# A hybrid decoder step: the S5 branch's inner table T kept in a contiguous layout

## The chip, the cores and the metric

The kernel runs on one core of a Trainium2 chip. The metric is the time of one execution in device microseconds; where several executions are given, their median. The trace is one execution, taken by the hardware profiler.

## What is computed

One layer of a hybrid decoder on 512 prompt tokens with 16 meta tokens in front, and on 8 running sequences of 4 tokens. After a norm and a large projection two branches run side by side: a gated linear recurrence in 8 heads (HGRN2), and a diagonal state-space branch (S5) in 64 groups of 16 channels with 64 complex states each. Their outputs are gated and merged; an expert-retrieval mixer (PEER) follows. The change touches the S5 branch:

```python
b_bar = ((a_bar - 1.0) / lam)[..., None] * lax.complex(b_re, b_im)
bu = jnp.einsum('gpc,nlgc->nlgp', b_bar, ug)
...
_, xs = lax.associative_scan(combine, (a_seq, bu), axis=1)
y = jnp.real(jnp.einsum('gcp,nlgp->nlgc', cc, xs)) + d_skip * ug
```

## The kernel before

The S5 branch is worked in blocks of 8 tokens. For each of the 64 groups a block's 8 x 16 = 128 inputs (U) give 128 outputs in two parts: one through the state at the start of the block (table W, 128x128 per group), and one directly from the inputs of the same block (table T, 128x128 per group, lower triangular in the tokens). A third table, AT, leads from the inputs into the state.

These tables are constants of the weights. `s5_setup` (L204) makes them on the chip, in 8 octets of 8 groups, and writes them to device memory as `Td`, `Wd` and `ATd`. It is a generator in the list `fill`: `Stream.run` calls `bg.tick` and `fill.tick` after every 12 of its matmuls, and each tick runs a generator up to its next `yield`. So the program order on every engine is set at build time, the set-up's steps lie between the matmuls of the weight stream (`gps`, L469) and the heads of the recurrence, and each engine then runs its instructions in that order. Transfers are issued with `load` (L104), nearly all on SP's queue, in program order too; a transfer whose data isn't ready holds those behind it. On the same queue are the weight tiles `wraw`, two buffers deep, each of which waits until POOL (or DVE) has read the tile before out of its buffer (`wl`, L435, after ACT's cast `wh`, L434).

For one octet the set-up computes E and W on DVE (L369, L371), multiplies E with C on PE (L382), adds the skip term on DVE (L378, L383) to give a small tile T7, transposes E on PE (L387) into AT, and then places T7 eight times, moved by 16 partitions each, with eight transfers into a tile T of shape [128, 2, 8, 16, 4]: half octet, token s, channel c, group g, with the group innermost. Two such tiles alternate between octets. They are cleared once by POOL (L342), and before that their space serves as the scratch u1, u2 of the complex multiplications (L255 to L260). `store` (L351) of an octet is called in the next octet's pass, just ahead of its L378, that of the last octet right after the last transfers.

In the same list `fill` a generator `rotations` runs on POOL (L276 to L298).

In `s5_units` (L700) 16 units of 4 groups each run as two interleaved generators in the list `bg`. A unit has four steps: loads and `px` (L745, AT with U); a swap of the halves by PE (`pxs`, L760) and a scan on DVE (L772); a second swap and the block states xs (L783, L784); and the output `py`, where T (L790) and W (L791) are the stationary operands of four groups and ACT takes the Gelu (L793). The matmuls are in float32 and each shows as two loads and two matmuls in the trace. T comes from `Td` as 512 contiguous elements per partition, group innermost, and is read through the view `p (n g) -> p g n`, so that neighbouring weights of a group lie four elements apart.

Of the kernel before, what the change touches and what calls it, by code (L numbers as in the profile page):

```python
# [8 lines left out]
F32 = mybir.dt.float32  # L9
# [10 lines left out]
P = 128  # L20
# [6 lines left out]
G = 64  # L27
# [63 lines left out]
def body(tc, a):  # L91
    nc = tc.nc
    mm = nc.tensor.matmul
    V, PO, AC = nc.vector, nc.gpsimd, nc.scalar
# [4 lines left out]
    def pool(st, name, bufs=1, right=False, space=None):  # L99
        kw = {} if space is None else {"space": space}  # L100
        return st.enter_context(tc.tile_pool(name=name, bufs=bufs, side="right" if right else "left", reuse_waits="tile", **kw))

    def load(dst, src):
        nc.sync.dma_start(dst, src)  # L104
# [90 lines left out]
    Td = dram.tile([8, P, 2, 4 * P], F32, name="Td")  # L195
# [8 lines left out]
    def s5_setup(pm, qr):  # L204
# [42 lines left out]
            V.tensor_scalar(c, c, -2.0, 1.0, ALU.mult, ALU.add)  # L247
        t1 = sm("t1")
        q = pool(s5, "s5c", 1, True)
        Ts = [q.tile([P, 2, 8, 16, 4], F32, name=f"T{i}") for i in range(2)]  # L250
        u1, u2 = (T.rearrange("p a s c g -> p (a s c g)")[:, : 4 * G].rearrange("p (n g) -> p n g", g=G) for T in Ts)

        def cmul(outr, outi, ar, ai, br, bi, n):
            a, b = u1[:, :n], u2[:, :n]
# [77 lines left out]
        for e in (1, 2, 4):  # L332
            o, i = slice(8 - 2 * e, 8 - e), slice(8 - e, 8)
# [4 lines left out]
        V.tensor_copy(s5c["a4s"][64:128], pim[64:128, 4])  # L338
        V.tensor_scalar(s5c["a4s"][0:64], pim[0:64, 4], -1.0, None, ALU.mult)

        for T in Ts:
            PO.memset(T, 0.0)  # L342

        def params(o):
            r = {}
# [3 lines left out]
            return r  # L349

        def store(o):  # L351
            load(Td[o], Ts[o % 2].rearrange("p a s c g -> p a (s c g)"))

        nx = params(0)
        yield
# [1 line left out]
        for o in range(8):  # L357
            gs = slice(8 * o, 8 * o + 8)
            p, nx = nx, (params(o + 1) if o < 7 else None)
            V.tensor_scalar(p["b2"], p["b2"], sgn, None, ALU.mult)  # L360
            V.tensor_scalar(p["ct1"], p["ct1"], nsgn, None, ALU.mult)
            V.tensor_scalar(p["ct2"], p["ct2"], -1.0, None, ALU.mult)
            AT = q.tile([P, 8, P], F32, name="AT", tag="AT", bufs=2)
            E = q.tile([P, 8, 8, 16], F32, name="E", tag="E")
            W = q.tile([P, 8, 8, 16], F32, name="W", tag="W", bufs=2)
            for x, u, w, cr, ci in ((E, "b1", "b2", gr[:, :, gs], gi[:, :, gs]), (W, "ct1", "ct2", pr[:, 1:, gs], pim[:, 1:, gs])):
                xv, tmp = x.rearrange("p g s c -> p s g c"), AT.rearrange("p g (s c) -> p s g c", s=8)
                for dst, pp, cc in ((xv, p[u], cr), (tmp, p[w], ci)):
                    V.tensor_tensor(dst, pp.unsqueeze(1).to_broadcast([P, 8, 8, 16]), cc.unsqueeze(3).to_broadcast([P, 8, 8, 16]), ALU.mult)  # L369
                    yield  # L370
                V.tensor_tensor(xv, xv, tmp, ALU.add)  # L371
                yield
            Ec = E.rearrange("p g s c -> p g (s c)")
            T7 = q.tile([P, 2, 16, 4], F32, name="T7", tag="T7")
            T7v = T7.rearrange("p a c g -> p a g c")
            if o > 0:
                store(o - 1)
            V.tensor_tensor(T7v, p["dsk"].rearrange("p (a g) c -> p a g c", a=2), ident[:, 112:128].unsqueeze(1).unsqueeze(1).to_broadcast([P, 2, 4, 16]), ALU.mult)  # L378
            yield
            pt = pm.tile([P, 8, 16], F32, name="pt", tag="m")  # L380
            for i in range(8):
                mm(pt[:, i], Ec[:, i], p["ct1"][:, i], start=True, stop=True)  # L382
            V.tensor_tensor(T7v, T7v, pt.rearrange("p (a g) c -> p a g c", a=2), ALU.add)  # L383
            for hf in range(2):
                pt = pm.tile([P, 4, P], F32, name="pt", tag="m")
                for i in range(4):
                    nc.tensor.transpose(pt[:, i], Ec[:, 4 * hf + i], ident)  # L387
                AC.copy(AT[:, 4 * hf : 4 * hf + 4], pt)
                yield
            load(Wd[o], W.rearrange("p g s c -> p g (s c)"))  # L390
            for s in range(8):
                load(Ts[o % 2][0 : 16 * (s + 1), :, s], T7[16 * (7 - s) : 128])
                if s % 2:
                    yield
            load(ATd[o], AT)
# [304 lines left out]
    def s5_units(ph, pm, sp, Ud, Yd, units):  # L700
# [25 lines left out]
        for n_, u in enumerate(units):  # L726
            o, hf = u // 2, u % 2
            g4 = slice(4 * hf, 4 * hf + 4)
            gs = slice(4 * u, 4 * u + 4)
            r, nxt = nxt, None  # L730
            U, rc, rs = r["U"], r["rc"], r["rs"]
            T, W, xs = st("T", P), st("W", P), st("xs", nxs)
            load(T.rearrange("p g n -> p (g n)"), Td[o][:, hf])
            T = T.rearrange("p g n -> p (g n)").rearrange("p (n g) -> p g n", g=4)
            load(W, Wd[o][:, g4])
            if ph.sample:
                xw0 = st("xw0", 8)
                load(xs[:, :, nch:nxs], a["x0"][:, gs])
                load(xw0, a["x0w"][:, gs])
            if n_ + 1 < len(units):  # L740
                nxt = loads(units[n_ + 1])
            px = pm.tile([P, 512], F32, name="px", tag="m")
            pxv = px[:, : 4 * nu].rearrange("p (g n) -> p g n", n=nu)
            for g in range(4):
                mm(pxv[:, g], r["AT"][:, g], U[:, g], start=True, stop=True)  # L745
            X = st("X", nu)
            AC.copy(X, pxv)
            d0 = st("d0", nch)
            PO.tensor_copy(d0, s5c["rho"][:, gs].unsqueeze(2).to_broadcast([P, 4, nch]))
            PO.memset(d0[:, :, 0:1], 0.0)  # L750
            if ph.first:
                PO.memset(xs[:, :, 0:1], 0.0)
            else:
                PO.tensor_copy(xs[:, :, 0], sstate[:, gs])
            yield

            def swap(src):
                t = pm.tile([P, 512], F32, name="pxs", tag="m")
                tv = t[:, : 4 * nch].rearrange("p (g n) -> p g n", n=nch)
                mm(tv, T_["perm"], src, start=True, stop=True)  # L760
                return tv

            xw = swap(X[:, :, :nch])
            Z, t2, z, zc = st("Z", nch), st("t2", nch), st("z", nch), st("zc", nch)
            V.tensor_tensor(Z, X[:, :, :nch], rc[:, :, 1 : nch + 1], ALU.mult)
            V.tensor_tensor(t2, xw, rs[:, :, 1 : nch + 1], ALU.mult)
            V.tensor_tensor(Z, Z, t2, ALU.subtract)
            if not ph.first:
                z0 = st("z0", 1)
                V.tensor_tensor(z0[:, :, 0], sstate[:, gs], s5c["rho"][:, gs], ALU.mult)  # L770
                V.tensor_tensor(Z[:, :, 0], Z[:, :, 0], z0[:, :, 0], ALU.add)
            V.tensor_tensor_scan(z.rearrange(fl), d0.rearrange(fl), Z.rearrange(fl), 0.0, ALU.mult, ALU.add)  # L772
            V.tensor_tensor(zc, z, rc[:, :, 1 : nch + 1], ALU.mult)
            if ph.sample:
                f, f2 = st("xf", 8), st("xf2", 8)
                PO.tensor_tensor(f, xs[:, :, nch:nxs], s5c["a4r"][:, gs].unsqueeze(2).to_broadcast([P, 4, 8]), ALU.mult)
                PO.tensor_tensor(f2, xw0, s5c["a4s"][:, gs].unsqueeze(2).to_broadcast([P, 4, 8]), ALU.mult)
                PO.tensor_tensor(f, f, f2, ALU.add)
                PO.tensor_tensor(f, f, X[:, :, nch + 8 : nch + 16], ALU.add)
                PO.dma_start(a["o_ssm_s"][:, gs], f)  # L780
            yield
            zw = swap(z)
            V.tensor_tensor(t2, zw, rs[:, :, 1 : nch + 1], ALU.mult)  # L783
            V.tensor_tensor(xs[:, :, 1:nch], zc[:, :, : nch - 1], t2[:, :, : nch - 1], ALU.add)  # L784
            V.tensor_tensor(sstate[:, gs], zc[:, :, nch - 1], t2[:, :, nch - 1], ALU.add)
            yield
            py = pm.tile([P, 512], F32, name="py", tag="m")
            pyv = py[:, : 4 * ny].rearrange("p (g n) -> p g n", n=ny)
            for g in range(4):
                mm(pyv[:, g], T[:, g], U[:, g, m0 : m0 + ny], start=True, stop=False)  # L790
                mm(pyv[:, g], W[:, g], xs[:, g, m0 : m0 + ny], start=False, stop=True)  # L791
            y = st("y", ny)
            AC.activation(y, pyv, AF.Gelu)  # L793
            AC.dma_start(Yd[o].rearrange("s c f -> (s c) f")[:, 4 * hf * ny : 4 * (hf + 1) * ny], y.rearrange(fl))
            yield
# [11 lines left out]
    def network(ph, keep_h2, wq, es, sq):  # L807
# [186 lines left out]
        if ph.first:  # L994
            lct = fill.add(late_consts())
            setup = fill.add(s5_setup(pm, pool(hd, "rot", 2)))
# [767 lines left out]
```

## Time and profile before

| | |
|---|---|
| median of 3 runs | 2227.87 us (2227.82 to 2234.36) |
| the profiled execution's own time | 2235.91 us |
| its span, first to last instruction | 2234.2 us |
| mean granted TensorE clock | 0.981 of full speed |
| busy share of the span: PE, DVE, ACT, POOL | 95%, 71%, 38%, 37% |
| S5 set-up, up to about | 435 us |
| S5 units, about | 500 to 662 us |

The span is cut into stretches because its stages differ: weight stream and heads up to about 500 us, the S5 units, then weight-stream matmuls, and the expert stages. How to read the rows below: a line of a group names the kernel's line, the engine, the operation and out<-in; PEld is the weight load, which overlaps PE. In a timeline the brackets tell how long the engine had been idle before the instruction and what ended that.

### The profile page before, as it was taken

The numbers are of one execution on the slowest core, as the hardware profiler recorded it, in microseconds if no ns is written. First come the engines' busy times: TensorE is split into PE (matmuls) and PEld (weight loads), VectorE is DVE, ScalarE is ACT, GpSimd is POOL, SyncE is SP. The second block draws the span as 40 slices with busy tenths as digits, with TensorE's granted clock in tenths as the row PEclk, the third lists the DMA queues.
The fourth block names the chain that finished last, engine by engine and source line by source line (L and its number), as shares of the span: only waits on it lengthen the run. The fifth ranks groups of instructions, "written<-read, shape, count | busy, mean of one in ns | idle before, by whom it ended". The sixth has DMA issues, their size and how long they took to land.

```text
span 2234.2 us, 34565 instructions
## 1 busy us (share of the span) xinstructions
PE 2112.2 (95%) x13085; PEld 1937.5 (87%) x13085; DVE 1578.4 (71%) x3056; ACT 848.8 (38%) x1583; POOL 815.8 (37%) x904
## 2 busy tenths in 40 slices
PE   7899998999999998999899999899999999999996
PEld 6889898898999998999799878788888888888885
DVE  6866566655445424799998778687778788777777
ACT  3323232333113324333477434343443433344343
POOL 3488762224443333664166111222222222222221
PEclk9999998999999999999999999999999999999998
DMA  4433344326644243232356979899889999888983
GB/s 147 121 111 119 123 126 137 113 100 186 200 134 129 88 151 121 81 109 68 111 227 260 332 276 331 308 335 334 326 309 333 334 331 333 309 330 312 331 300 148
DMA packets 199814, 478.90 MB, mean 214 GB/s; under 512 B 53440, under 2 KB 114752, under 8 KB 176096
## 3 DMA queue, kind: packets, MB, share of 16 engines
q1 hardware_dynamic: 169136, 278.50, 37.6%
q0 software_dynamic: 24752, 170.67, 20.3%
q10 hardware_dynamic: 5760, 27.53, 3.1%
q8 instruction: 103, 1.69, 0.3%
q14 instruction: 63, 0.52, 0.1%
HBM read 419.42 MB, written 54.46 MB: 212 GB/s over the span
## 4 chain that ended last, share of the span: by engine, by line
PE 53%; DVE 26%; issue 8%; ACT 7%; DMA 5%; POOL 1%; SPq 0%; DVEq 0%; POOLq 0%; ACTq 0%
PE gps L469 23%; PE eacc L1548 7%; DVE uv L1353 5%; DVE tlo L1477 5%; PE hps L1493 3%; PE hps L1495 3%; PE hps L1494 3%; DVE acc L1360 3%; ACT thi L1469 3%; PE pw L1428 3%; DMA traw<-in_uv 2%; DVE glo L483 2%; PE aps L605 1%; ACT w L1355 1%; PE py L790 1%
## 5 line engine op out<-in xcount | busy, mean ns | idle before, releaser
L469 PE MATMUL gps<-pr,wh 128*128 128x272 f32 (+1 forms) x3328 | 584.7, 298 | 5.8 <-DVE pr L483 3.2
L469 PEld LDWEIGHTS gps<-pr,wh 128*128 128x128 f32 x3328 | 481.7, 192 | 14.5 <-issue 4.4
L1477 DVE TENSOR_TENSOR tlo<-traw,thi 128x1024 fp32r<-128x1024 f32 x241 | 298.9, 1241 | 146.3 <-ACT thi L1469 146.3
L1339 POOL DMA_INDIRECT uv<-in_uv,ei x128 | 176.4, 1378 | 605.4 <-DVE acc L1360 578.1
L469 PE MATMUL gps<-pr,wl 128*128 128x272 f32 (+1 forms) x1664 | 354.4, 293 | 8.8 <-POOL wl L435 7.7
L1495 PE MATMUL hps<-pr,tlo 128*128 128x384 f32 x1024 | 348.5, 340 | 15.0 <-DVE tlo L1477 13.5
L1493 PE MATMUL hps<-pr,thi 128*128 128x384 f32 x1024 | 350.8, 343 | 8.6 <-ACT thi L1469 8.6
L435 POOL TENSOR_TENSOR wl<-wraw,wh 128x1024 fp32r<-128x1024 f32 x88 | 216.9, 2465 | 350.8 <-ACT wh L434 338.9
L1494 PE MATMUL hps<-pr,thi 128*128 128x384 f32 x1024 | 344.5, 336 | 0.0
L1469 ACT CAST thi<-traw 128x1024 fp32r<-128x1024 f32 x256 | 266.1, 1040 | 44.5 <-DMA traw<-in_uv 15.6
L469 PEld LDWEIGHTS gps<-pr,wl 128*128 128x128 f32 x1664 | 267.3, 192 | 9.9 <-POOL wl L435 8.2
L1548 PE MATMUL eacc<-thi,ghi 128*128 128x512 f32 x768 | 243.7, 398 | 10.6 <-ACT ghi L482 9.4
L1548 PE MATMUL eacc<-tlo,ghi 128*128 128x512 f32 x768 | 243.4, 398 | 4.1
L1548 PE MATMUL eacc<-thi,glo 128*128 128x512 f32 x768 | 238.5, 392 | 0.0
L1360 DVE SCALAR_TENSOR_TENSOR acc<-uv,w,acc 128x1024 f32<-128x1024 f32 x158 | 202.3, 1280 | 30.5 <-ACT w L1355 30.5
L1354 ACT ACTIVATE w<-w 128x1 f32<-128x1 f32 x160 | 32.5, 203 | 486.3 <-DVE uv L1353 486.3
L1495 PEld LDWEIGHTS hps<-pr,tlo 128*128 128x128 f32 x1024 | 192.9, 188 | 23.0 <-DVE tlo L1477 21.8
L1493 PEld LDWEIGHTS hps<-pr,thi 128*128 128x128 f32 x1024 | 193.4, 189 | 15.8 <-ACT thi L1469 10.7
L1494 PEld LDWEIGHTS hps<-pr,thi 128*128 128x128 f32 x1024 | 193.4, 189 | 3.6
L1353 DVE SCALAR_TENSOR_TENSOR uv<-uv,h 128x1024 f32<-128x1024 f32 x160 | 194.8, 1217 | 0.0
L1548 PEld LDWEIGHTS eacc<-tlo,ghi 128*128 128x128 f32 x768 | 141.9, 189 | 50.1 <-DVE tlo L1477 21.9
L1548 PEld LDWEIGHTS eacc<-thi,ghi 128*128 128x128 f32 x768 | 141.2, 189 | 46.6 <-ACT ghi L482 22.6
(405 smaller groups left out, 3021.5 us busy)
## 6 DMA issues: line engine op xcount, KB each, us to landing
traw<-in_uT SPq DMA_DIRECT2D x128, 512.0 KB
traw<-in_uv SPq DMA_DIRECT2D x128, 512.0 KB
wraw<-in_W SPq DMA_DIRECT2D x104, 512.0 KB
Wt<-wb ACTq DMA_DIRECT2D x24, 1024.0 KB
wt<-Wt SPq DMA_DIRECT2D x15, 1536.0 KB
st<-in_state_hgrn SPq DMA_DIRECT2D x8, 512.0 KB
Wd<-W SPq DMA_DIRECT2D x8, 512.0 KB
ATd<-AT SPq DMA_DIRECT2D x8, 512.0 KB
```

The lines of the kernel that those rows point to most:

```text
L435: E.tensor_tensor(wl, r3, wh, ALU.subtract)
L469: mm(ps[:, b, :w], x[:, k], y[:, k, b * w : b * w + w], start=(k == 0 and x is wh and y is hi), stop=(k == KT - 1 and x is wl))
L1339: PO.indirect_dma_start(out=uvs[j], out_offset=None, in_=a["uv"], in_offset=bass.IndirectOffsetOnAxis(ap=ei[:, k : k + 1], axis=0))
L1353: V.scalar_tensor_tensor(out=uv[:, 0:D], in0=uv[:, 0:D], scalar=1.0, in1=h2, op0=ALU.mult, op1=ALU.mult, accum_out=w)
L1360: V.scalar_tensor_tensor(acc, uv[:, D:], w, acc, ALU.mult, ALU.add)
L1428: mm(pt[:, t], o2[:, t], o1[:, t], start=True, stop=True)
L1469: AC.copy(x, t)
L1477: (PO if kind == "u" and e < sum(AQ) else V).tensor_tensor(y, raws.pop((kind, e)), x, ALU.subtract)
L1493: mm(ps[:, :nt], x[:, ks], hi[:, k, cs], start=(k == 0), stop=False)
L1494: mm(ps[:, :nt], x[:, ks], lo[:, k, cs], start=False, stop=False)
L1495: mm(ps[:, :nt], y[:, ks], hi[:, k, cs], start=False, stop=(k == KT - 1))
L1548: mm(accs[d][:, b], l[:, ds_], r[:, b * 512 : b * 512 + 512], start=st, stop=en)
```

## The change

The two tiles T become one, and a second tile Tc of the same size holds the octet in the order half octet, group, (s c). The store first copies T into Tc on ACT, with a step of four elements in the source, and writes Tc to `Td`. The unit reads T from `Td` as before, but without the regrouping view. The scratch u1, u2 lies in the one T, and there is one memset.

```diff
--- before.py
+++ after.py
@@ -247,8 +247,10 @@
             V.tensor_scalar(c, c, -2.0, 1.0, ALU.mult, ALU.add)
         t1 = sm("t1")
         q = pool(s5, "s5c", 1, True)
-        Ts = [q.tile([P, 2, 8, 16, 4], F32, name=f"T{i}") for i in range(2)]
-        u1, u2 = (T.rearrange("p a s c g -> p (a s c g)")[:, : 4 * G].rearrange("p (n g) -> p n g", g=G) for T in Ts)
+        T = q.tile([P, 2, 8, 16, 4], F32, name="T")
+        Tc = q.tile([P, 2, 4, P], F32, name="Tc")
+        Tf = T.rearrange("p a s c g -> p (a s c g)")
+        u1, u2 = (Tf[:, 4 * G * i : 4 * G * (i + 1)].rearrange("p (n g) -> p n g", g=G) for i in range(2))
 
         def cmul(outr, outi, ar, ai, br, bi, n):
             a, b = u1[:, :n], u2[:, :n]
@@ -338,8 +340,7 @@
         V.tensor_copy(s5c["a4s"][64:128], pim[64:128, 4])
         V.tensor_scalar(s5c["a4s"][0:64], pim[0:64, 4], -1.0, None, ALU.mult)
 
-        for T in Ts:
-            PO.memset(T, 0.0)
+        PO.memset(T, 0.0)
 
         def params(o):
             r = {}
@@ -349,7 +350,8 @@
             return r
 
         def store(o):
-            load(Td[o], Ts[o % 2].rearrange("p a s c g -> p a (s c g)"))
+            AC.copy(Tc, T.rearrange("p a s c g -> p a g (s c)"))
+            load(Td[o], Tc.rearrange("p a g n -> p a (g n)"))
 
         nx = params(0)
         yield
@@ -389,7 +391,7 @@
                 yield
             load(Wd[o], W.rearrange("p g s c -> p g (s c)"))
             for s in range(8):
-                load(Ts[o % 2][0 : 16 * (s + 1), :, s], T7[16 * (7 - s) : 128])
+                load(T[0 : 16 * (s + 1), :, s], T7[16 * (7 - s) : 128])
                 if s % 2:
                     yield
             load(ATd[o], AT)
@@ -731,7 +733,6 @@
             U, rc, rs = r["U"], r["rc"], r["rs"]
             T, W, xs = st("T", P), st("W", P), st("xs", nxs)
             load(T.rearrange("p g n -> p (g n)"), Td[o][:, hf])
-            T = T.rearrange("p g n -> p (g n)").rearrange("p (n g) -> p g n", g=4)
             load(W, Wd[o][:, g4])
             if ph.sample:
                 xw0 = st("xw0", 8)
```

## Rows read from the trace of the kernel before

**Rows 1.** Busy time by stretch around the S5 units: engine busy us (x instructions)
```profile
core 0: us, PE busy (x) PEld busy (x) DVE busy (x) ACT busy (x) POOL busy (x), PEclk, DMA share, GB/s
560.00:580.00 20.00, 20.00 (x143) 19.76 (x141) 7.75 (x18) 3.68 (x6) 9.89 (x19) 1.00 0.67 204
...
580.00:600.00 20.00, 18.43 (x133) 17.65 (x131) 9.19 (x18) 3.44 (x6) 8.27 (x18) 1.00 0.64 195
```

**Rows 2.** PE groups by line and shape, 500 to 662: busy us, mean ns
```profile
L790 PE MATMUL py<-s_U,s_T 128*128 128x72 f32 x128 | 39.2, 388 | 0.0
...
L790 PEld LDWEIGHTS py<-s_U,s_T 128*128 128x128 f32 x128 | 34.8, 320 | 0.4 <-issue 0.2
...
L791 PE MATMUL py<-s_xs,s_W 128*128 128x72 f32 x128 | 25.2, 279 | 0.4 <-DVE s_xs L784 0.4
...
L791 PEld LDWEIGHTS py<-s_xs,s_W 128*128 128x128 f32 x128 | 20.8, 202 | 0.5 <-DVE s_xs L784 0.5
...
L745 PEld LDWEIGHTS px<-s_U,s_AT 128*128 128x128 f32 x128 | 15.4, 192 | 0.0
```

**Rows 3.** Chain of waits in order of time, 500 to 670: start, us, what
```profile
595.61 0.41 PE py L790 x2
...
596.92 0.46 PE py L790 x2
...
598.07 0.22 PE py L791 x2
...
598.30 1.55 PE gps L469 x12
...
604.08 0.85 PE px L745 x8
```

**Rows 4.** PE's waits, 500 to 662: us in total, times, longest us
```profile
PE pxs L760 <- DVE s_z L772: 4.2, 6, 1.3
```

**Rows 5.** PE's waits in the set-up, 100 to 440 us
```profile
PE gps L469 <- POOL wl L435: 7.0, 1, 7.0
...
PE aps L612 <- ACT h_sq L627: 2.0, 4, 0.8
```

**Rows 6.** Timeline around the memsets and PE's wait for wl
```profile
98.69 1.84 POOL L342 MEMSET T<- 128x1024 f32 x2 [3.57 <-DVE gi L260]
...
106.47 0.21 POOL L288 TENSOR_TENSOR rc<-u,u 128x8 f32<-128x8 f32 x1
...
106.74 1.22 DVE L369 TENSOR_TENSOR E<-d_b,gr 128x1024 f32<-128x1024 f32 x1
...
106.76 1.26 POOL L291 TENSOR_TENSOR u<-rc,rs 128x8 f32<-128x8 f32 x1
...
106.79 1.04 ACT L434 CAST wh<-wraw 128x1024 fp32r<-128x1024 f32 x1
...
110.39 3.32 POOL L435 TENSOR_TENSOR wl<-wraw,wh 128x1024 fp32r<-128x1024 f32 x1
...
113.77 0.83 PE L469 MATMUL gps<-pr,wl 128*128 128x280 f32 x2 [7.02 <-POOL wl L435]
```

**Rows 7.** ACT groups by line and shape, whole run
```profile
L434 ACT CAST wh<-wraw 128x1024 fp32r<-128x1024 f32 x104 | 108.5, 1044 | 13.4 <-PE gps L469 10.8 <-DMA wraw<-in_W 2.2 <-ACT s_y L793 0.5
...
L1430 ACT COPY wb<-pw 128x1024 f32<-128x1024 f32 x48 | 48.3, 1008 | 22.1 <-PE pw L1428 19.6 <-DMA Wt<-wb 2.3
```

**Rows 8.** Timeline: transfers into T of octets 4 and 7, and what follows
```profile
331.23 6.06 SPq L104 DMA_DIRECT2D T<-T  x8
...
349.83 0.39 DVE L378 TENSOR_TENSOR T<-d_dsk,c_ident 128x128 f32<-128x128 f32 x1
...
429.39 2.64 SPq L104 DMA_DIRECT2D T<-T  x4
...
433.65 0.41 ACT L627 COPY h_sq<-f_kB 128x256 f32<-128x256 f32 x1 [7.12 <-DVE f_kB L625]
...
434.59 0.33 SPq L104 DMA_DIRECT2D Td<-T  x1
```

## The prediction

> **What bounds the kernel now.** I read the page first (PE busy 95% of the span), then the busy time by stretch around the S5 branch, because that is where the changed table is used. From 500 to 662 us the 16 units of `s5_units` run between the matmuls of the weight stream, and PE is busy for 18.4 to 20.0 us of a stretch of 20 us, at a granted clock of 1.00, that is at the 2.4 GHz level; DVE, ACT and POOL are at half or less [rows 1]. So PE's own work is what this stage lasts, and the reader should see in rows 1 that there is hardly a gap in which a cheaper matmul could get lost. Next I read the costs by line and shape in the same stretch [rows 2]. L790 multiplies with the table T and L791 with W. Both have the same shape (128x128 stationary, 72 moving columns, 128 executions), yet a weight load of L790 takes 320 ns against 202, and its matmul 388 ns against 279. A load of L745, with AT as stationary operand, takes 192 ns. What sets L790 apart is that its stationary operand is read with a step of four elements (16 bytes): the view `p (n g) -> p g n` that the change drops. The chain of waits shows the same by distance [rows 3]: in a `py` group two L790 matmuls take 0.46 us and two L791 take 0.22 us; a whole group (8 and 8) runs from 595.61 to 598.30, 2.69 us, while 8 matmuls of L745 take 0.85 us. Busy times overlap, distances on the chain don't, and both say that the price is paid on PE's path.
>
> The set-up of the tables (100 to 440 us) is the other place. There PE is held now and then by DVE, once for 7.0 us by POOL, and by ACT hardly at all: 2.0 us in four waits [rows 5].
>
> **The change, part by part.**
>
> *The contiguous weight load.* 128 loads of L790 become loads like those of L791. By the load's mean: 128 x (320 - 202) ns = 15.1 us. By the matmul's mean: 128 x (388 - 279) = 14.0 us. By distance: 16 groups x (2.69 - 2 x 0.85) = 15.8 us. I take 15.1, with 14.0 and 15.8 as ends; they agree because PE is saturated.
>
> What is late next? A round of both unit streams takes about 20 us and would take about 18. Each unit needs its DVE scan (L772) between two swaps on PE, and here PE already waits: 4.2 us in six waits, 1.3 us at most [rows 4]. No `py` group lies between these swaps in the order of the work, so their distance should stay; but the phase against POOL's and DVE's other work moves. If every one of the 8 rounds got one such wait anew, 8 x 1.3 = 10.4 us would go back. I take 1.5 us given back, near the one wait that the row shows at its longest, with 0 and 10.4 as ends. Net gain of this part 13.6 us (3.6 to 15.8). After 662 us PE runs weight-stream matmuls without a break, so an earlier end of the stage moves everything behind it.
>
> *One memset instead of two.* `PO.memset` of the second T goes. The two stand on POOL from 98.69 for 1.84 us [rows 6], so 0.95 us goes. POOL is behind there: rotation work, then `wl` L435 at 110.39, and that is what PE waits 7.02 us for, until 113.77. So this part is on the path. It may be worth more than its length: the rotation step L291 took 1.26 us, and the like two behind it stretched until 110.39, against 0.21 us for L288 just before, since DVE's large L369 started at 106.74 next to L291 at 106.76. Started 0.95 us earlier, they end before it; `wl` could then start when ACT's cast ends (106.79 + 1.04 = 107.83) instead of at 110.39, 2.5 us sooner. I take 2.0 us gained, between 0.95 and 2.5, nearer the upper end because the rows' start times are that close.
>
> *Eight copies on ACT.* `store` now issues an `AC.copy` of 128x1024 elements with a step in its source. The trace of before has no copy from SBUF with this step. Nearest are L434 (128x1024, contiguous, 1044 ns) and L1430 (128x1024 from PSUM, stepped, 1008 ns) [rows 7]. So 8 x 1.04 = 8.3 us of ACT time is the upper end if each copy delays PE by all of its length; the lower end is 0, since work added to an engine cannot by itself speed up PE here. The cover is ACT's idle time: PE's waits for ACT in the whole set-up are 2.0 us [rows 5], and for seven of the eight copies the data has long been there: the smallest distance is octet 4, whose transfers into T were issued by 331.23 + 6.06 = 337.29, while the DVE step that follows the store in the program ran at 349.83 [rows 8]. I take 0.5 us lost. Without that cover it would be the 8.3.
>
> About the source's step a page of the Trainium skill has something that speaks against the change: SBUF - State Buffer, in the note on "cachelines" of the section on the DMA port swizzle, says that accesses which go to a new 16-byte line each time pay a penalty. The rows on L790 fit that; by it the penalty would also meet the new copy. If it were as large as that of the weight load (320 to 202), a copy would take 1.65 us, eight 13.2 us, and the sum's upper end for this part would be that instead of 8.3; no row of before shows ACT under it.
>
> *The last copy.* For octet 7 the store follows the transfers at once. They leave SP's queue at 429.39 and last 2.64 us, ATd follows, and the store of Td went out at 434.59, when they had landed [rows 8]. Before, only SP waited there. Now ACT waits in its own order, and behind the copy stand `h_sq` L627 (at 433.65, then needed by PE's L612), the Tanh L877 and the cast `wh` L434. L627 would start at about 434.6 + 1.04 = 435.6, 1.9 us later. Ends 0 (another DVE wait hides it) and 1.9 + 1.04 = 2.9 us; I take 1.5 us lost, since DVE is the later one soon after.
>
> *The rest* costs nothing: the Td store has the same size, SP waits for ACT instead of for the transfers alone (behind it on SP stand weight loads that mostly wait for POOL's `wl` anyway), and T as a single buffer is free again as soon as ACT has copied it, several steps before the next transfers into it.
>
> *Sum:* -13.6 - 2.0 + 0.5 + 1.5 = -13.6 us. Against the profiled execution (2235.91 us, of which 2234.2 are its span and 1.7 lie around it) that gives 2222.3. This execution is 8.0 us above the median of the runs shown, 2227.87 (2227.82 to 2234.36), so against the median the forecast is 2214.3 us, 0.61% less.
>
> **The rivals.**
>
> *The stage gives it back.* PE's 15.1 us are saved, but the rounds are then set by the scan on DVE or by unit loads queued on SP behind weight loads. For it: the six waits in rows 4. Against it: PE has no more than 1.6 us of gap in any stretch of rows 1, and DVE is half idle. With all 10.4 us given back and the gain at its lower end: -3.6 - 2.0 + 2.0 = -3.6, 2224.3 us. Chance 0.15.
>
> *The copies stall ACT, and ACT stalls PE: slower.* Place: the eight copies in the set-up, ACT executing in order with the evictions and casts of the stream behind them. If each cost what the last one may, 2.9 us, that is 23.5, and with 15.6 gained the result is +7.9, 2235.8 us. It decides from 15.6 / 8 = 1.95 us per copy. Against it stands the distance in rows 8. Chance 0.05.
>
> *The weight load is hidden or its price is not the layout.* Then L790 keeps its distance, and only set-up terms are left, -2.0 + 2.0 = 0: 2227.9 us. For it: weight loads run beside matmuls, and the long matmul of L790 could in principle come from its moving operand U. Against it: L745 has the same U as moving operand, contiguous weights, and 0.85 us for 8 [rows 2, 3]; two L790 take twice as long as two L791. Chance 0.06. The page TensorE: Matmul & The Clock Gate of the Trainium skill (What happens when you issue a matmul) says that the next weights load while the running matmul streams, by which a longer load would be covered; with 72 columns to stream the rows show it is not.
>
> **How the numbers follow.** Forecast 0.74, rivals 0.15, 0.05 and 0.06. Predicted 2214.3 us. The best ends together are -15.8 - 2.5 = -18.3, 2209.6 us, and I go to 2208 for the spread between runs. Upwards the worst ends together would be +6.7 (2234.5), which needs all of them at once; I stop at 2224, where the first rival's time begins, which leaves out the most of the three rivals' 0.26 above and keeps a little of it inside, some 0.2 in all. A measurement of this kernel can tell about 0.3% from no change, 6.7 us. Faster than that: nearly all of the forecast and a fifth of the first rival, 0.75. Within: the rest of these and the third rival, 0.20. Slower: 0.05.
>
> **What would show it.** In the profile after, L790 should have L791's numbers, about 200 ns for the load and 280 for the matmul; a `py` group should take about 1.7 us; the stage should end some 14 us sooner after its start. If L790 is shorter and the stage is not, the waits of PE for s_z must have grown. At 98.7 us there should be one memset, and PE's wait for `wl` before 114 us should be 1 to 2.5 us shorter. The copies should take about 1.04 us each, seven of them without a wait for transfers; the eighth should hold ACT near 430 us. The prediction is wrong if L790 stays at 320 ns, or if PE's waits for ACT in the set-up exceed 10 us.

## The result, and the profile after

| | kernel before | changed kernel |
|---|---|---|
| median, same chip, 10 runs each | 2229.58 us (2222.71 to 2234.36) | 2219.19 us (2208.44 to 2225.05) |
| ratio | | 0.9946 [0.9931, 0.9962] |
| profiled execution, and its span | 2235.91 us, 2234.2 us | 2218.1 us, 2216.3 us |
| granted TensorE clock | 0.981 | 0.980 |

The changed kernel is faster by 0.54% (0.38 to 0.69), 12.0 us by the ratio and 10.4 between the medians; the forecast was 13.6 us or 0.61%. Lines from L352 on have moved by one or two numbers: the two halves of a `py` group are now L791 (table T) and L792 (W), the cast is L436, `wl` L437, the streamed matmul L471, and the new copy L353.

First the S5 stage, where the gain was expected. The groups by line and shape, 495 to 652 us (instructions, busy us, mean ns, as in [rows 2]):

```profile
L792 PE MATMUL py<-s_xs,s_W 128*128 128x72 f32 x128 | 25.1, 278 | 0.0
L791 PE MATMUL py<-s_U,s_T 128*128 128x72 f32 x128 | 24.6, 274 | 0.0
L791 PEld LDWEIGHTS py<-s_U,s_T 128*128 128x128 f32 x128 | 20.2, 196 | 0.4 <-DVE s_t L784 0.2
L792 PEld LDWEIGHTS py<-s_xs,s_W 128*128 128x128 f32 x128 | 19.8, 195 | 0.2 <-DVE s_xs L785 0.2
```

The load of T went from 320 to 196 ns and its matmul from 388 to 274 [rows 2]: L791 can no longer be told from L792. The load of W fell a little too, from 202 to 195. On the chain of waits (start, us, what) one group reads:

```profile
595.31 0.17 PE py L791 x2
595.48 0.22 PE py L792 x2
595.71 0.22 PE py L791 x2
...
597.05 1.56 PE gps L471 x12
598.61 0.85 PE px L746 x8
```

From 595.31 to 597.05 the group takes 1.74 us; it took 2.69 [rows 3]. Two L791 cost what two L792 cost, 0.22 us (the first two of the group 0.17), and the `px` group kept its 0.85. The stage from the first `px` matmul to the last `py` matmul lasted 159.7 us before and lasts 146.8 now, 12.9 less; the granted clock from 500 to 660 us was 0.99 in both. PE is as full as before, and what it waits for is what it waited for (a stretch: us, then busy us and count of PE, PEld, DVE, ACT, POOL, granted clock, DMA share, GB/s; under them PE's wait, us in total, times, longest):

```profile
560.00:580.00 20.00, 20.00 (x162) 19.73 (x162) 7.23 (x18) 4.34 (x8) 11.00 (x25) 1.00 0.68 206
```

```profile
PE pxs L761 <- DVE s_z L773: 4.3, 6, 1.3
```

Now the set-up. PE's waits from 100 to 440 us (as in [rows 5]), and the timeline around the memset (as in [rows 6]; the bracket is the idle time before the instruction and what ended it):

```profile
PE aps L614 <- ACT h_sq L629: 5.0, 5, 2.7
PE gps L471 <- POOL wl L437: 4.2, 2, 3.3
```

```profile
97.81 0.95 POOL L343 MEMSET T<- 128x1024 f32 x1 [2.72 <-DVE gi L262]
...
106.10 1.21 DVE L371 TENSOR_TENSOR E<-d_b,gr 128x1024 f32<-128x1024 f32 x1
106.17 1.21 POOL L295 TENSOR_TENSOR rs<-u,u 128x8 f32<-128x8 f32 x1
...
107.34 3.32 POOL L437 TENSOR_TENSOR wl<-wraw,wh 128x1024 fp32r<-128x1024 f32 x1
...
110.72 0.72 PE L471 MATMUL gps<-pr,wl 128*128 128x280 f32 x2 [3.34 <-POOL wl L437]
```

One memset of 0.95 us stands where 1.84 us of two stood, and one rotation step of POOL is drawn out beside DVE's large product (L295, 1.21 us), where three were before. PE's longest wait for `wl` is 3.3 us instead of 7.0; the 7.0 is itself high, for four other profiles with two memsets of T have 5.3 to 5.5. The wait for ACT has gone from 2.0 to 5.0 us. The copy itself, by its tile (ns: shortest, median, longest; first and last start), and the last one on the timeline:

```profile
L353 ACT COPY Tc<-T x8: 1987/2056/2079, 173.9 to 430.4; 128x1024 f32<-128x1024 f32 x8
...
  DMA T<-T: 8.2, 1
```

```profile
425.10 2.64 SPq L104 DMA_DIRECT2D T<-T  x4
...
430.45 1.99 ACT L353 COPY Tc<-T 128x1024 f32<-128x1024 f32 x1 [8.20 <-DMA T<-T]
...
432.80 0.71 PE L614 MATMUL aps<-h_qF,h_sq 128*128 128x128 f32 x4 [2.67 <-ACT h_sq L629]
```

A copy takes 2.06 us, about twice the 1.04 of the cast [rows 7]. ACT stood for 8.2 us in front of the last one, until the four transfers had landed; `h_sq` L629 is behind it in ACT's order, and PE waited 2.67 us for that. This is the place and the kind of wait that [rows 8] had led to.

A caution for all that follows: one profile is one execution. The set-up's length moves by some 4 us either way between profiles of kernels that don't differ there, and the profiled execution of before is 6.3 us above its median here (2235.91 to 2229.58). So differences of a few us far from the edit are not read from a single pair, and the last 6.7 of the pair's 17.8 us, which arise after 661 us, are left to this spread.

### The profile page after: what moved, and what is told of

The parts are those of the page before. It is cut to its first block, busy times and chain, and to the rows that moved or that the text cites. A ratio compares the mean times of both kernels' runs of the same rounds, so it can differ in the third digit from the quotient of the medians.

```text
span 2216.3 us, 34598 instructions
## 1 busy us (share of the span) xinstructions
PE 2099.9 (95%) x13085; PEld 1925.7 (87%) x13085; DVE 1571.2 (71%) x3056; ACT 865.0 (39%) x1591; POOL 815.7 (37%) x903
## 4 chain that ended last, share of the span: by engine, by line
PE 42%; DVE 20%; issue 7%; ACT 6%; DMA 4%; POOL 1%; SPq 0%; DVEq 0%; POOLq 0%; ACTq 0%
PE gps L471 16%; PE eacc L1549 8%; DVE uv L1354 5%; DVE tlo L1478 5%; PE hps L1496 4%; PE hps L1494 4%; PE hps L1495 4%; DVE acc L1361 3%; ACT thi L1470 3%; PE pw L1429 3%; DVE glo L485 2%; DMA traw<-in_uv 1%; DMA traw<-in_uT 1%; ACT w L1356 1%; DVE o L1409 1%
## 5 line engine op out<-in xcount | busy, mean ns | idle before, releaser
L471 PE MATMUL gps<-pr,wh 128*128 128x272 f32 (+1 forms) x3328 | 585.9, 298 | 5.7 <-DVE pr L485 3.8
L471 PEld LDWEIGHTS gps<-pr,wh 128*128 128x128 f32 x3328 | 482.2, 192 | 14.4 <-DVE pr L485 4.6
L1496 PE MATMUL hps<-pr,tlo 128*128 128x384 f32 x1024 | 349.5, 341 | 13.6 <-DVE tlo L1478 12.2
L471 PE MATMUL gps<-pr,wl 128*128 128x272 f32 (+1 forms) x1664 | 354.2, 293 | 6.0 <-POOL wl L437 4.8
L437 POOL TENSOR_TENSOR wl<-wraw,wh 128x1024 fp32r<-128x1024 f32 x88 | 218.4, 2482 | 343.9 <-ACT wh L436 336.5
L471 PEld LDWEIGHTS gps<-pr,wl 128*128 128x128 f32 x1664 | 267.8, 192 | 7.3 <-POOL wl L437 5.5
```

The lines of the kernel that those rows point to most:

```text
L437: E.tensor_tensor(wl, r3, wh, ALU.subtract)
L471: mm(ps[:, b, :w], x[:, k], y[:, k, b * w : b * w + w], start=(k == 0 and x is wh and y is hi), stop=(k == KT - 1 and x is wl))
L1496: mm(ps[:, :nt], y[:, ks], hi[:, k, cs], start=False, stop=(k == KT - 1))
```

## The experiments

All ratios are to the kernel before, on the same chip, with a 95% interval.

**The load alone.** The view that regroups T's columns is dropped, with no copy: the matmuls get contiguous loads of a table in another column order.

```diff
-            T = T.rearrange("p g n -> p (g n)").rearrange("p (n g) -> p g n", g=4)
```

> The kernel before with the regrouping view of T in the unit dropped, and nothing else: two tiles T, two memsets, no copy. The elements of T that reach PE are then in the wrong order, so the direct part of the S5 output is left out as a result; the work is the same. Theory (the step of the stationary operand is what costs in the S5 stage): a load of the T matmul takes about 195 ns instead of 320, a py group about 1.76 us instead of 2.69, and the time is 13 to 15 us below before (ratio 0.993 to 0.994). Rival (the price comes from the moving operand U or is covered): loads stay near 320 ns, ratio 1.000.

2213.73 us (2211.17 to 2220.66), ratio 0.9941 [0.9919, 0.9963], 13.2 us by the ratio (8.3 to 18.1). In its rows of the tile `py` (ns: shortest, median, longest) the load of T is L789:

```profile
L789 PEld LDWEIGHTS py<-s_U,s_T x128: 186/192/192, 509.8 to 640.9; 128*128 128x128 f32 x128
```

192 ns, and a stage of 143.8 us instead of 159.7. The contiguous load alone gives as much as the whole change, so the rest of the change should come to about nothing or to a small loss.

**All but the load.** The changed kernel with the regrouping view put back: one memset, one T and the copies, and the step in the load (the columns again in another order).

```diff
             load(T.rearrange("p g n -> p (g n)"), Td[o][:, hf])
+            T = T.rearrange("p g n -> p (g n)").rearrange("p (n g) -> p g n", g=4)
```

> The changed kernel with the regrouping view put back into the unit, so that the weight loads are stepped again; the copies on ACT, the one T and the one memset stay. The direct part of the S5 output is again in the wrong order. It shows the set-up's share alone. Theory from the trace of the changed kernel (about 4 us gained before 420 us, some 5.7 us lost between 420 and 474 us at the last copy): first px matmul about 1.8 us later than before, time 0 to 4 us above before (ratio 1.000 to 1.002). Rival (the copies cost nothing and the whole forecast gain of the memset arrives): 2 us below before, ratio 0.999. With the view alone the two should add up to the change.

2231.44 us, ratio 1.0013 [0.9996, 1.0029]: 2.9 us slower, with no change just inside the interval.

```profile
L792 PEld LDWEIGHTS py<-s_U,s_T x128: 307/322/333, 511.7 to 658.2; 128*128 128x128 f32 x128
```

The load has its 322 ns again, the stage its length (161.4 us), and ACT stood 8.2 us for the transfers as in the changed kernel. The two halves add up within their intervals: -0.59 + 0.13 = -0.46%, against -0.54% for the whole. The first `px` matmul was expected 1.8 us later than before and came 4.6 us earlier (497.2 against 501.8 us), so from that start alone the set-up's share can't be read.

**Half the step.** The kernel before, with T read at a step of two elements (8 bytes) instead of four.

```diff
-            T = T.rearrange("p g n -> p (g n)").rearrange("p (n g) -> p g n", g=4)
+            T2 = T.rearrange("p g n -> p (g n)").rearrange("p (a n g) -> p a g n", a=2, g=2)
...
-                mm(pyv[:, g], T[:, g], U[:, g, m0 : m0 + ny], start=True, stop=False)
+                mm(pyv[:, g], T2[:, g // 2, g % 2], U[:, g, m0 : m0 + ny], start=True, stop=False)
```

> The kernel before with a view of T whose neighbouring weights lie two elements (8 bytes) apart instead of four; the direct part of the S5 output is in the wrong order. Theory (a load is slow where each element lies in another 16-byte piece): loads of the T matmul at about 195 ns, as without a step. Rival (any step costs): 250 to 320 ns.

One run, 2219.87 us; the load of T is L790 here:

```profile
L790 PEld LDWEIGHTS py<-s_U,s_T x128: 194/197/333, 512.6 to 646.9; 128*128 128x128 f32 x128
```

197 ns: a step of 8 bytes is as good as none (192), and one of 16 bytes costs 322. So the price does not grow evenly with the step; it is there at 16 bytes and not at 8. The Trainium skill, SBUF - State Buffer, in the note on cachelines, says that two hits on a 16-byte line are enough for full bandwidth. At 8 bytes two elements lie on a line, at 16 one, and the 197 and 322 ns agree with that.

**The last copy later.** Eight steps of the other work are let past before the store of octet 7, so that ACT meets the copy when the transfers have landed.

```diff
+        for _ in range(8):
+            yield
         store(7)
```

> The changed kernel with eight yields ahead of the last store, so that the copy of octet 7 stands some 15 us later in ACT's order and its transfers have landed. Theory (the loss at the last copy is ACT standing 8.2 us for the transfers, 2.7 us of PE waiting for ACT and the fall of the granted clock behind it): ACT waits for no transfer, PE's wait for h_sq near 430 us is below 0.5 us, the granted clock from 436 to 480 us is 1.00, and the time is 4 to 6 us below the changed kernel, that is about 16 us below before (ratio 0.992 to 0.993). Rival (the loss is the length of the copies): the same as the changed kernel, ratio 0.9946.

2214.26 us, ratio 0.9937 [0.9916, 0.9958]. Timeline:

```profile
428.45 0.71 PE L616 MATMUL aps<-h_qF,h_sq 128*128 128x128 f32 x4 [0.15 <-ACT h_sq L631]
...
434.71 2.04 ACT L353 COPY Tc<-T 128x1024 f32<-128x1024 f32 x1
```

The copy has no idle time in front of it, and PE waits 0.15 us where it waited 2.67; all its waits for ACT in the set-up come to 2.3 us, near the 2.0 of before [rows 5]. So the wait was the place of the copy in ACT's order and not its length, which is the same 2.04 us. The granted clock from 436 to 480 us was 1.00, as expected. The time is less clear: a ratio of 0.992 to 0.993 was expected, and the interval around 0.9937 holds the changed kernel's 0.9946 too, so what the wait is worth in the kernel's time needed a second comparison (below).

**The step on the other side.** The copy reads T in order and writes with the step. This kernel was built on the one before it, so it has the eight steps ahead of the last store too, which its expectation doesn't mention; the length of a copy, for which it was run, isn't touched by that.

```diff
-            AC.copy(Tc, T.rearrange("p a s c g -> p a g (s c)"))
+            AC.copy(Tc.rearrange("p a g n -> p a n g"), T.rearrange("p a s c g -> p a (s c) g"))
```

> The changed kernel with the copy turned round: it reads T in the order in which it lies and writes Tc with the step (neighbouring elements 128 elements apart in Tc). Theory (the 2.06 us of the copy come from reading each element out of another 16-byte piece, as with the weight load): a copy takes about 1.04 us, as the contiguous cast does. Rival (ACT pays for a step on either side): it stays near 2.06 us. The time of one run tells nothing here.

One run, 2211.41 us:

```profile
L353 ACT COPY Tc<-T x8: 1979/2040/2092, 173.4 to 434.0; 128x1024 f32<-128x1024 f32 x8
```

2.04 us: nothing is won. Against the contiguous cast of 1.04 us the step costs ACT about 1.0 us on 128x1024 elements on whichever side it stands, though the writes here go 512 bytes apart and the reads there went 16. No contiguous copy of this size was run; two smaller copies of the kernel before that read whole runs, L1433 (128x128, 298 ns) and L627 (128x256, 406 ns), give an estimate of 1.05 us for it by their difference, which supports the cast as the measure.

**A second memset, of Tc.** To give back the POOL time that the change saved:

```diff
+        PO.memset(Tc, 0.0)
         PO.memset(T, 0.0)
```

> The changed kernel with a second memset of the same size on POOL ahead of that of T. Theory (the memset stands on the path to the wl that PE waits for, and its absence also moves the rotation steps ahead of DVE's large products): POOL's wl near 107 us starts 0.9 to 3 us later than in the changed kernel, at 108.2 to 110.4, and PE's matmul that waited until 110.72 starts at 111.6 to 113.8. Rival (the earlier start came from elsewhere): it starts at 110.7 still.

One run, 2217.36 us. It told nothing on the question:

```profile
93.44 0.96 POOL L343 MEMSET Tc<- 128x1024 f32 x1
...
97.07 0.95 POOL L344 MEMSET T<- 128x1024 f32 x1 [2.68 <-DVE gi L262]
...
108.33 3.32 POOL L438 TENSOR_TENSOR wl<-wraw,wh 128x1024 fp32r<-128x1024 f32 x1
```

Tc was free earlier than T, so its memset ran at 93.44, in a gap, and POOL still waited 2.68 us for DVE before T's. The saved 0.95 us was not given back. A memset of T itself, below, can't move into that gap.

**The change once more, and a version without copy.** On another chip the changed kernel was measured beside one that puts the columns in order where they are made: T7 and T carry the group ahead of the column, the transfers write the final order, and there are two T and two memsets as before, and no copy.

```diff
-        Ts = [q.tile([P, 2, 8, 16, 4], F32, name=f"T{i}") for i in range(2)]
+        Ts = [q.tile([P, 2, 4, 8, 16], F32, name=f"T{i}") for i in range(2)]
...
-            T7 = q.tile([P, 2, 16, 4], F32, name="T7", tag="T7")
+            T7 = q.tile([P, 2, 4, 16], F32, name="T7", tag="T7")
...
-                load(Ts[o % 2][0 : 16 * (s + 1), :, s], T7[16 * (7 - s) : 128])
+                load(Ts[o % 2][0 : 16 * (s + 1), :, :, s], T7[16 * (7 - s) : 128])
...
-            T = T.rearrange("p g n -> p (g n)").rearrange("p (n g) -> p g n", g=4)
```

> The changed kernel itself, beside the next one on the same chip, so that the two compare directly. Expected as on record: ratio to before 0.9946, 2.0 to 2.1 us for each copy, ACT standing 8.2 us at the last.

> The contiguous table without a copy: T7 and the two tiles T hold the group outside the channel, so that T lies in the unit's order at once; the eight transfers into T then move 16 contiguous elements at a time (64 bytes) instead of 64 (256 bytes); two memsets, nothing new on ACT. Theory (the S5 stage's gain is the layout's, and the set-up's cost is the copy's): the gain of the view alone, 13 to 17 us below before (ratio 0.9925 to 0.994), PE's waits for ACT in the set-up as before (about 2 us). Rival (four times as many pieces per transfer make the transfers late, and weight tiles queue behind them): PE waits for wl more than 7 us in the set-up, and the time is at or above that of the changed kernel.

The change: 2220.7 us, 0.9971 [0.9957, 0.9985]. Without copy: 2214.19 us, 0.9938 [0.9926, 0.995]; the intervals don't meet. Its waits of PE from 100 to 440 us, and its transfers into T:

```profile
PE gps L469 <- POOL wl L435: 5.4, 1, 5.4
PE aps L612 <- ACT h_sq L627: 1.8, 3, 0.8
```

```profile
L104 SPq DMA_DIRECT2D T<-T x64: 595/647/1679, 131.4 to 425.1; - x64
```

The wait for ACT is 1.8 us, no more than before the change [rows 5], and issuing a transfer into T keeps SP's queue for 647 ns at the median (637 before). The stage is 144.0 us. So the layout can be had at the transfers for next to nothing in time, though not in packets: from 100 to 440 us the DMA engines handled 54206 instead of 26468, and their busy share was 0.43 instead of 0.39. On the same chip this version is 6.5 us faster than the change. Part of that 6.5 may be a weak showing of the change on this chip (0.9971 here, 0.9946 and 0.996 elsewhere): the mean granted clock of its 12 runs averages 0.9793, against 0.9813 for the runs of the kernel before and 0.9805 for this version.

**T's memset twice.**

```diff
         PO.memset(T, 0.0)
+        PO.memset(T, 0.0)
```

> The changed kernel with T's own memset issued twice, so that the second waits like the first for the last scratch product and can't run in a gap of POOL as the added one of the run with two memsets did. Theory (the memset that the change drops is on the path to the wl that PE waits for): PE's wait for wl ends at 113.3 to 113.8 us, as in the four profiles with two memsets of T, against 109.9 to 111.7 in the profiles with one, and the first pt matmul of the set-up starts at 127.3 to 127.7 instead of 123.9 to 125.9. Rival (the earlier start belongs to the one tile as scratch): it ends by 111.7.

One run, 2219.09 us:

```profile
97.01 0.95 POOL L343 MEMSET T<- 128x1024 f32 x1 [2.71 <-DVE gi L262]
...
98.02 0.95 POOL L344 MEMSET T<- 128x1024 f32 x1
...
112.10 0.83 PE L472 MATMUL gps<-pr,wl 128*128 128x280 f32 x2 [5.51 <-POOL wl L438]
```

PE starts at 112.10, earlier than expected, because everything here was 1.7 us earlier than in the profile of before. Counted from the first memset's start it is 112.10 - 97.01 = 15.09 us, and before 113.77 - 98.69 = 15.08 [rows 6]. The distance tells more than the time of day, and it can be read in every profile. With two memsets in a row (before, the load alone, half the step, no copy, and this one) it is 14.8 to 15.1 us. With one it is 12.7 to 12.9 in six profiles (12.91 in the changed kernel) and 14.5 to 14.7 in three. The memset's own start differs too: 98.3 to 98.7 us in the four profiles with two tiles T, 97.0 to 98.3 in the ten with one, 1.0 us earlier on average. That part can't come from the memset that was dropped; it goes with the one tile as scratch, the rival named here, and its cause is not shown.

**Every copy twice.** The kernel with the later last copy, each copy doubled, beside that kernel and the change again, all on one chip.

```diff
+            AC.copy(Tc, T.rearrange("p a s c g -> p a g (s c)"))
             AC.copy(Tc, T.rearrange("p a s c g -> p a g (s c)"))
```

> The kernel with the last copy later, and each of the eight copies on ACT done twice: 8 x 2.05 = 16.4 us more of ACT time in the set-up. Theory (a copy whose data is there is covered by ACT's idle time): within 3 us of the kernel with the last copy later. Rival (copies delay PE through ACT's order by about their length): 8 to 16 us slower than that kernel.

> The kernel with the last copy later again, beside the changed kernel on the same chip. Theory: 4 to 6 us below the changed kernel, ratio to before 0.992 to 0.9935. Rival: the same as the changed kernel, 0.995 to 0.997.

> The changed kernel on the same chip as the last two, for the direct comparison: ratio to before between 0.9946 and 0.9971, the two values had so far.

Copies twice: 2228.17 us, 0.9996 [0.9983, 1.0008]. Last copy later: 2217.6 us, 0.9946 [0.993, 0.9961]. The change: 2219.42 us, 0.996 [0.9945, 0.9975]. Eight more copies, 16.4 us of ACT's time, cost 10.6 us between the medians of the first two. The expectation that ACT's idle time would take them in fell. PE's wait behind the last pair, and the stretch in which it stands:

```profile
PE po L674 <- ACT h_Sc L666: 2.2, 1, 2.2
```

```profile
436.00:460.00 24.00, 21.17 (x121) 18.87 (x121) 8.33 (x17) 9.16 (x18) 6.04 (x3) 0.79 0.19 66
```

From the last transpose of the set-up (L387 in the kernel before) to the last `pos` matmul (L678) this profile takes 78.1 us; the two of the single-copy kernel take 69.8 and 69.8. So 8.3 of the 10.6 us fall there, around the last pair (442.4 to 446.5) and in a stretch whose granted clock was 0.79, that is partly at the 1.2 GHz level. A low clock is not peculiar to this one profile: the mean granted clock of the kernel's 12 runs averages 0.9773, against 0.9798 for the single-copy kernel and 0.9804 for the kernel before on the same chip. Within a kernel, a run with a mean clock lower by 0.001 is some 1.7 us longer (129 runs), so by an estimate some 4 of the 10.6 us go with the lower clock. As the two kernels differ in the copies alone, that clock is their doing too; by what way is not shown. The seven pairs ahead of it, from the first product of E with C (`pt`, L382 in the kernel before) to the last transpose, cost between 1.2 and 6.7 us by the same profiles (293.7 against 292.5 and 287.0), which settles nothing.

The third run of the change has the same stall as its first, some 8 us later:

```profile
438.68 1.99 ACT L353 COPY Tc<-T 128x1024 f32<-128x1024 f32 x1 [8.60 <-DMA ATd<-AT]
...
441.02 0.71 PE L614 MATMUL aps<-h_qF,h_sq 128*128 128x128 f32 x4 [3.04 <-ACT h_sq L629]
```

By the times, taking it away is worth 1.8 us between the medians on this chip (2219.42 - 2217.6) or 3.1 by the ratios, less than the 4 to 6 expected, and the intervals overlap.

## Why the prediction was right, and where its terms were off

**The weight load: right.** 128 loads and matmuls became like W's, as the sum had it, and the half step and the load alone show that the cause is the 16-byte step. The sum took 13.6 us net. Measured: 12.9 us by the stage in the pair of profiles, 13.2 by the times of the load alone, and 11.4 to 15.9 in other profiles with the contiguous or the half step (stages of 148.3 to 143.8 us; 150.2 with the copies doubled). That range mixes clocks: eight stages of 143.8 to 144.6 us had a granted clock of 1.00 from 500 to 660 us, the four of 146.8 to 150.2 one of 0.97 to 0.99, and the two with the 16-byte step (159.7 and 161.4) one of 0.99. The forecast had read a clock of 1.00 and half-idle DVE for the whole stage; in the kernel before the clock was 0.95 and 0.96 from 500 to 540 us, and DVE was busy for 15.8 of the first 20 us. A group became 2.69 - 1.74 = 0.95 us shorter, 16 of them 15.2 us, which is the 15.1 of the sum; of this 12.9 arrived in the pair, and 14.6 against the other profile with the step. No wait of PE in the stage grew to account for the rest, so the 1.5 that I took as given back is not shown.

**The stage gives it back: fell.** PE's wait for `s_z` is 4.3 us in six waits, as before [rows 4]. The scan lies between two swaps, no `py` group is between these, and nothing took PE's place as the bound.

**The load is hidden: fell.** The load alone moved the kernel by 13.2 us.

**The memset: right in size on average, wrong as one number.** I argued that POOL's rotation steps would end ahead of DVE's large product and `wl` would start up to 2.5 us sooner, and took 2.0. In the pair the wait ends 15.08 - 12.91 = 2.2 us sooner after the memset. Over all profiles there are two cases: 2.2 us in six, some 0.5 in three, 1.6 on average. The mechanism is seen in both: in the pair one rotation step was drawn out, in the second profile of the change, which is one of the three, it was three steps of 1.07 us each. It lives from two start times that lie close, and such a term should have been told as two values with a chance each. The first product of E with C behind it (`pt`) starts at 127.3 to 127.7 us in four of the profiles with two memsets (126.3 in that of T's memset twice) and at 125.6 on average with one (123.9 to 128.5), 1.9 us sooner. That 1.9 holds the 1 us or so that is there at the memset's start already and that the forecast did not have; so it is the set-up's head start as a whole, and it came near the 2.0 in part by luck.

**The length of a copy: mis-sized by two.** The sum had 8 copies of 1.04 us, after a contiguous copy from SBUF and a stepped one from PSUM [rows 7]; measured 2.06. Neither row goes through SBUF element by element with a step; the copy from PSUM writes there in runs of eight. The sentence on the Trainium skill, SBUF - State Buffer, had the direction right: its estimate of 1.65 us was nearer than my rows. The point from which the copies would make the change slower was 1.95 us *lost* per copy; the copies are longer than that, and the change is still faster, because most of their length is covered. From the first product of E with C to the last transpose, the four profiles without copies take 285.6 to 291.7 us (mean 287.7) and those with single copies 285.5 to 294.4 (mean 289.4): some 1.7 us for seven copies, no more than the spread, where I took 0.5.

**The last copy: right place, too cheap.** I took 1.5 us with ends 0 and 2.9. ACT's stand of 8.2 us was foreseen in kind, the 2.67 us of PE's wait lie near the upper end, and that end would have been higher with the true length of the copy. From the last transpose to the last `pos` matmul, profiles with the stall take 73.8 us on average (72.4 to 75.4, six) and those without it 70.4 (69.4 to 72.2, seven): 3.4 us.

In the pair alone this place seems to cost more. PE is 4.3 us ahead of before at the last transpose and 1.5 behind at the last L607 (L605 before), 5.8 us lost. Part of it is the clock, 1.00 before and lower after. Changed kernel, then no copy, then the change's third run:

```profile
436.00:460.00 24.00, 23.53 (x169) 21.52 (x169) 9.39 (x22) 7.37 (x19) 7.54 (x4) 0.93 0.19 66
460.00:480.00 20.00, 18.53 (x137) 18.04 (x138) 11.35 (x28) 3.38 (x11) 2.50 (x1) 0.91 0.16 53
```

```profile
414.00:436.00 22.00, 20.01 (x147) 19.44 (x147) 14.04 (x27) 6.86 (x15) 6.88 (x3) 0.92 0.48 132
436.00:460.00 24.00, 24.00 (x175) 21.87 (x174) 8.40 (x23) 7.05 (x17) 4.75 (x2) 0.93 0.19 66
```

```profile
436.00:460.00 24.00, 20.27 (x152) 18.32 (x151) 10.91 (x22) 8.98 (x20) 6.88 (x3) 1.00 0.26 93
```

It is tempting to say that PE's stall let the clock fall. But the kernel without a copy has no such stall and 0.92 and 0.93, and the third run of the change has the stall at 441.02 and 1.00 from 414 to 500 us. Over all profiles but that of the doubled copies, the clock was below 1.00 somewhere in these stretches in three of the six with the stall and in three of the seven without. So the fall in the pair is not shown to come from the copy, and 3.4 us is the number to keep.

**The sum again.** With measured terms, and the load alone by its times: -13.2 - 1.9 + 1.7 + 3.4 = -10.0 us. The three measurements of the change gave -12.0, -6.5 (0.9971 of 2228.93) and -8.9 (0.996 of 2228.18). All but the load should cost -1.9 + 1.7 + 3.4 = +3.2 us and was measured at +2.9. The forecast's 13.6 lies above two of the three because the copies were taken at half their length and the last one at less than half its price; it was the first measurement, the best of the three, that came close to it, and that closeness is partly luck. The 2214.3 us lies 4.9 below the measured median: 1.7 of it is the median of before, which was 2229.58 with ten runs, and the other 3.2 the two terms named.

**Open.** How much the last copy costs in the kernel's time: 1.8 to 3.1 us by the one direct comparison, 3.4 by the profiles. Why the three measurements of the change run from 0.9946 to 0.9971, with intervals that just overlap; the weakest has the change's lowest mean clock (0.9793, against 0.9804 in the other two), and why it was lower there is not known. How the doubled copies bring the lower clock. And why the set-up's memset starts earlier with the one tile.

## What to carry to other kernels

Compare a matmul's weight load with that of a neighbour of the same shape: a difference such as 320 to 192 ns can be a layout to be mended, and where PE was full, as here, nearly all of its length came back. Mend it where the data is made, for here the right order at the transfers cost no measurable time while a copy on another engine gave back a part; and if it must be a copy, look for the one copy that has to wait for a transfer, since it holds up everything behind it in its engine's order. Price a stepped copy by a stepped row, and a gain that hangs on two close start times by two values.

## What the runs showed of the hardware

A weight load of 128x128 f32 takes 192 ns contiguous, 197 at a step of 8 bytes and 320 to 322 at a step of 16. An ACT copy of 128x1024 f32 between SBUF tiles takes 2.06 us with a step of 16 bytes in its source and 2.04 with a step of 512 bytes in its destination, twice the 1.04 us of the contiguous cast; that the side doesn't matter was not expected. Small POOL steps of 0.21 us took 1.07 to 1.26 us beside DVE's products of 128x1024. The granted clock between 414 and 480 us came out at 0.91 to 1.00 in different executions of the kernels without doubled copies, without a link to the stall in front of it, and with the doubled copies the mean clock of 12 runs averaged 0.9773 instead of 0.9798.
